# Seven half chunks of weights at another distance from the streamed tiles, and new paddings, in a two-block float32 network

## The chip, the cores and the metric

The kernel runs on one core of a Trainium2 chip. What counts is the device time of one execution in microseconds, the median of several runs. All times below are of that kind, or come from one profiled execution, in which they are counted from the start of its span.

## What is computed

Everything is float32, for one sequence of 256 tokens of width 1024. A first block (gated delta net, then a mixture of 16 experts) hands its normed result to a second block, which is the part that the change touches:

```python
def second_block(x, ...):
    for l in range(2):
        x = x + 0.5 * swiglu_ffn(rms_norm(x, g_ffn1[l]), w_up1[l], w_down1[l])
        h = rms_norm(x, g_mix[l])
        z = h @ w_in[l]          # z_lx, z_lg, q, k, v, f_logit, gates
        xr = causal_depthwise_conv(z_lx, conv_w[l], conv_b[l])
        hr = rg_lru(xr, w_a[l], b_a[l], w_x[l], b_x[l], lam[l])
        y_lru = (gelu(z_lg) * hr) @ w_lru_out[l]
        o = forgetting_attention(q, k, v, f_logit, g_q[l], g_k[l])
        y_attn = o @ w_attn_out[l]
        x = x + (gate_lru * y_lru + gate_attn * y_attn) @ w_o[l]
        x = x + 0.5 * swiglu_ffn(rms_norm(x, g_ffn2[l]), w_up2[l], w_down2[l])
    return x

def swiglu_ffn(h, w_up, w_down):       # w_up: 1024 x 5632, w_down: 2816 x 1024
    gate, up = split(h @ w_up, 2)
    return (silu(gate) * up) @ w_down
```

## The kernel before

**Three matmuls for one.** Each float32 operand is split into two fp32r parts, hi and lo, whose sum is the value. `mm3` (lines 238 to 243) issues three matmuls for every product of a 128x128 block of weights with 256 columns of activations: hi by hi (L241), lo weights by hi (L243 in the page, `mm<-xh,wlo`) and hi weights by lo (L242, `mm<-xl,whi`). The activations are the streamed (moving) operand, the weights are loaded. The scheduler issues the three in turn, so on TensorE nothing but such matmuls follow each other for long stretches.

**Weights.** They come in chunks of 128x2048 floats, 1 MB each, in the order that `order` gives: for each layer ffn1 (22 chunks `up1`, 11 of `down1`), the mix (`w_q`, `w_k`, `w_v`, `w_lx` for four groups, then `w_lg`, `w_g`, `w_la`, `w_o`), and ffn2 as ffn1. A chunk is loaded by one DMA on SyncE's queue into a `ring` of three, and `split` (L218) cuts it into two halves: for each, ScalarE writes `whi` (L228) and VectorE `wlo` (L229), from four places each. A half chunk feeds 24 matmuls. `weights` keeps two chunks ahead of their use. One ffn is 22 x 48 + 11 x 48 = 1584 matmuls.

**Streamed tiles.** `norm` writes `xh` (ScalarE, L254) and `xl` (VectorE, L255) per block of 128 channels, right after the residual add that makes this block (in w_o that is L726, `x<-mm,x`), and sums the squares on GpSimd (L259); a matmul with ones (L264, `ss<-sums,pack_base`) then gives the norm, behind the first chunk of the next stage. In ffn, `hh` and `hl` are the streamed tiles of `down`. In the mix, `w_lg` runs while the softmax of the last attention group is still worked on; its products go to one of three PSUM banks and L675 takes each out (`b<-mm,rstd`), which frees the bank for a later product.

**Other matmuls in fp32r.** `vproj` (L745 to L747) has the roles swapped: `xh` or `xl` is loaded and the weights are streamed. In `attention`, 8 matmuls for each of four groups (L566) spread the norms by `selt`, a matrix of zeros and ones that is the loaded operand. Some small products are in fp32: the scores (L579, L581: `qz`, `kz`) and `wax` (L646).

**Places.** The program fixes the address of every tile. `homed` pads the streamed tiles with 256 floats and lets them start 192 bytes into the padding; a padding `even` ahead of the pools sets the rest. Taken modulo 512, `xh`, `xl`, `hh`, `hl` and the streamed tiles of the mix all start at 352 and all `whi` and `wlo` at 160: weights 192 bytes below. For `vproj` it is the same pair the other way round. `selt` and `rn` lie at a distance of 128, `kz` and `qz`, `wax` and `xr` at 0.

**Order.** A scheduler lays out each engine's instructions from the dependencies and from when places come free. A new `whi` can be written when the last matmul that reads its place (four half chunks ago) is done.

Of the kernel before, what the change touches and what calls it, by code (L numbers as in the profile page):

```python
# [10 lines left out]
F32 = mybir.dt.float32  # L11
# [4 lines left out]
P = 128  # L16
T = 256
# [146 lines left out]

HOME, WEIGHTS = 192, 160


def homed(pool, n, dt, **kw):  # L170

    t = pool.tile([P, n * T + 256], dt, **kw)
    return t[:, HOME // 4:HOME // 4 + n * T].rearrange("p (k n) -> p k n", k=n)


class Kernel:
# [43 lines left out]
    def split(self, pool, raw, bufs=4, places=None):  # L220

        nc = self.nc
        parts = []
        for i in range(2):
            hi, lo = places[i]() if places else (pool.tile([P, 1024], F32R, tag=t, bufs=bufs, name=self.uid(t))
                                                 for t in ("whi", "wlo"))
            r = raw[:, 1024 * i:1024 * (i + 1)]
            nc.scalar.activation(hi, r, AF.Copy)  # L228
            nc.vector.tensor_sub(lo, r, hi.bitcast(F32))  # L229
            parts.append((hi, lo))  # L230

        def cols(n, size=P):
            i, o = divmod(n, 1024)
            return parts[i][0][:, o:o + size], parts[i][1][:, o:o + size]

        return cols
# [8 lines left out]
    def norm(self, x, g):  # L245

        nc, wp = self.nc, self.wp
        xh = homed(wp, KD, F32R, tag="xh", bufs=1, name=self.uid("xh"))
        xl = homed(wp, KD, F32R, tag="xl", bufs=1, name=self.uid("xl"))
        sums = wp.tile([P, T], F32, tag="sums", bufs=1, name=self.uid("sums"))  # L250

        def step(k):
            sq = wp.tile([P, T], F32, tag="t1", bufs=6, name=self.uid("sq")) if k else sums
            nc.scalar.activation(xh[:, k], x[:, k], AF.Copy, scale=self.c(g, k))  # L254
            nc.vector.scalar_tensor_tensor(xl[:, k], x[:, k], self.c(g, k), xh[:, k].bitcast(F32),  # L255
                                           op0=ALU.mult, op1=ALU.subtract)
            nc.scalar.activation(sq, x[:, k], AF.Square)
            if k:
                nc.gpsimd.tensor_add(sums, sums, sq)  # L259

        def finish():

            ss = self.ps.tile([P, 512], F32, tag="sm", bufs=2, name=self.uid("ss"))
            nc.tensor.matmul(ss[:, :T], self.cc["ones"], sums, start=True, stop=True)  # L264
            rms = wp.tile([P, T], F32, tag="t1", bufs=6, name=self.uid("rms"))
            nc.scalar.activation(rms, ss[:, :T], AF.Sqrt, bias=self.eps, scale=1.0 / D)
            rstd = wp.tile([P, T], F32, tag="rstd", bufs=2, name=self.uid("rstd"))
            nc.vector.reciprocal(rstd, rms)
            return rstd

        return ks(xh), ks(xl), step, finish

    def opening(self, x, f, g):

        nc, wp = self.nc, self.wp
        fg = self.wp1.tile([P, KD], F32, name="fg")
        nc.vector.tensor_mul(fg, self.cs(f), self.cs(g))

        by = self.wp1.tile([P, KD, 2], F32, name="by")
        nc.vector.memset(by[:, :, 0], 1.0)  # L280
        nc.vector.tensor_mul(by[:, :, 1], self.cs(f), self.cs(f))
        xh = homed(wp, KD, F32R, tag="xh", bufs=1, name=self.uid("xh"))
        xl = homed(wp, KD, F32R, tag="xl", bufs=1, name=self.uid("xl"))
        ss = self.ps.tile([P, 512], F32, tag="sm", bufs=2, name=self.uid("ss"))
        for k in range(KD):
            nc.scalar.activation(xh[:, k], x[:, k], AF.Copy, scale=fg[:, k:k + 1])
            nc.vector.scalar_tensor_tensor(xl[:, k], x[:, k], fg[:, k:k + 1], xh[:, k].bitcast(F32),
                                           op0=ALU.mult, op1=ALU.subtract)
            sq = wp.tile([P, T], F32, tag="t1", bufs=6, name=self.uid("sq"))
            nc.scalar.activation(sq, x[:, k], AF.Square)  # L290
            for t in range(2):
                nc.tensor.matmul(ss[:, 2 * t:2 * t + 2], sq[:, t * P:(t + 1) * P], by[:, k],
                                 start=(k == 0 and t == 0), stop=(k == KD - 1), skip_group_check=True)

        def spread(r):

            t = wp.tile([P, T], F32, tag="t1", bufs=6, name=self.uid("t"))
            tv = t.rearrange("p (t n) -> p t n", t=2)
            nc.vector.tensor_copy(tv, r[:, :, None].to_broadcast([P, 2, P]))
            b = self.ps.tile([P, 512], F32, tag="sm", bufs=2, name=self.uid("b"))  # L300
            for t in range(2):
                nc.tensor.matmul(b[:, t * P:(t + 1) * P], tv[:, t], self.cc["ident"], start=True, stop=True)
            return b[:, :T]

        def finish():
            sv = ss[:, :4].rearrange("p (t i) -> p i t", t=2)
            r = self.wp1.tile([P, 2, 2], F32, name="r")
            nc.scalar.activation(r[:, 0], sv[:, 0], AF.Sqrt, bias=self.eps, scale=1.0 / D)
            nc.vector.reciprocal(r[:, 0], r[:, 0])
            nc.vector.tensor_mul(r[:, 1], sv[:, 1], r[:, 0])  # L310
            nc.vector.tensor_mul(r[:, 1], r[:, 1], r[:, 0])
            nc.scalar.activation(r[:, 1], r[:, 1], AF.Sqrt, bias=self.eps, scale=1.0 / D)
            nc.vector.reciprocal(r[:, 1], r[:, 1])
            nc.vector.tensor_mul(r[:, 1], r[:, 1], r[:, 0])
            rstd = wp.tile([P, T], F32, tag="rstd", bufs=2, name=self.uid("rstd"))
            nc.scalar.activation(rstd, spread(r[:, 1]), AF.Copy)
            self.pending = residual(r[:, 0])
            return rstd

        def residual(r):  # L320
            rms = wp.tile([P, T], F32, tag="sums", bufs=1, name=self.uid("rms"))
            nc.scalar.activation(rms, spread(r), AF.Copy)
            for k in range(KD):
                yield
                nc.vector.scalar_tensor_tensor(x[:, k], x[:, k], self.c(f, k), rms, op0=ALU.mult, op1=ALU.mult)

        return ks(xh), ks(xl), None, finish

    def ffn(self, l, j, x, norm, g, out=None):

        nc, d = self.nc, self.d
        with ExitStack() as es:
            hp = self.pool("ffn", 1, ctx=es)
            xh, xl, _, finish = norm
            hh = homed(hp, FFT, F32R, name="hh")
            hl = homed(hp, FFT, F32R, name="hl")
            for m in range(FFT):
                w = self.weights(f"up{j}", l * FFT + m)
                pg = self.bank()
# [46 lines left out]
    def weights(self, name, i):  # L386

        while len(self.ahead) < 2:
            n = next(self.chunks, None)
            if n is None:  # L390
                break
            self.ahead.append((n, self.split(self.wp, self.load(self.d[n[0]][n[1]]))))
        n, w = self.ahead.pop(0)
        assert n == (name, i)
        return w
# [4 lines left out]
    def block2(self, x, out):  # L400
        nc = self.nc
        with ExitStack() as es:
            self.wp = self.pool("wp", 2, ctx=es)
            self.wp.tile([P, WEIGHTS // 4], F32, tag="even", bufs=1, name="even")
            self.ps = self.pool("ps", 1, True, ctx=es)
            self.wp1 = self.pool("wp1", 1, ctx=es)
            self.unpack("block2", self.wp1)
            self.selt = self.wp1.tile([P, 512], F32R, name="selt")

            self.wp1.tile([P, 64], F32, name="even")  # L410
            rows = self.cc["ident"].rearrange("p (n s) -> p n s", n=4)[:, :, :2]
            for n in range(4):
                nc.scalar.activation(self.selt[:, n * P:(n + 1) * P].rearrange("p (s c) -> p s c", c=64),
                                     rows[:, n, :, None].to_broadcast([P, 2, 64]), AF.Copy)
            self.chunks, self.ahead, self.pending = self.order(), [], iter(())
            norm = self.opening(x, "final_g", "g_ffn10")
            for l in range(LAYERS):
                norm = self.ffn(l, 1, x, norm, f"g_mix{l}")
                norm = self.mix(l, x, norm)
                norm = self.ffn(l, 2, x, norm, f"g_ffn1{l + 1}" if l + 1 < LAYERS else None, out)  # L420

    def mix(self, l, x, norm):
        nc, d, wp, ps = self.nc, self.d, self.wp, self.ps
        with ExitStack() as es:
            mp = self.pool("mix", 1, ctx=es)

            def big(i, dt=F32):
                return homed(mp, KD, dt, tag=f"b{i}", bufs=1, name=self.uid(f"b{i}"))

            def t1():  # L430
                return wp.tile([P, T], F32, tag="t1", bufs=6, name=self.uid("t"))
# [70 lines left out]
                tick()  # L502

            live.append(tokens())

            tmp("even", (P, 48))
            hr, lg = big(0), big(1)
            gh, gl, oh, ol = (big(i, F32R) for i in (2, 3, 4, 5))
            cv = [t.rearrange("(t two) n -> t two n", two=2) for t in (cum, ncum)]
# [1070 lines left out]
```

## Time and profile before

| what | us |
|---|---|
| median of three runs | 2606.05 |
| the three runs | 2598.6, 2606.05, 2613.8 |
| the profiled execution | 2613.88 |
| its span | 2612.2 |
| TensorE busy | 2255.4 (86%) |
| VectorE busy | 1203.8 (46%) |
| ScalarE busy | 982.7 (38%) |
| GpSimd busy | 278.9 (11%) |
| all `wlo` splits (460, VectorE) | 584.3 |
| all `whi` splits (460, ScalarE) | 484.6 |

The first block takes the first 1312 us or so; its second half is bound by the DMA of the experts' weights. Behind it, the second block runs at about half the DMA share. In the rows below a line reads: start in us, length in us, engine, line, operation, output<-inputs, and in brackets the idle time ahead of it with what ended it. Lengths of matmuls overlap, since TensorE is pipelined: the distance from start to start is what a matmul costs, and it is read from rows some places apart.

### The profile page before, as it was taken

To read this page: it belongs to the slowest core of one execution; us is meant where nothing else is said; L and a number is where in the kernel's file an instruction comes from. 1 tells how busy PE (TensorE), PEld (TensorE's weight loads), DVE (VectorE), ACT (ScalarE), POOL (GpSimd) and SP (SyncE) were. 2 spreads that over 40 slices of the span, in tenths; PEclk is the share of its full clock that TensorE was granted. 3 is DMA by queue.
4 is the path that set the end of the run, shared out by engine and by line. 5 is a ranking of instruction groups with operands and counts; after the bars stand their busy time and mean duration, and the time that the engine had idled before them with its cause. 6 is when DMAs were issued, how large, how long until landed. Compare 5 with 4: busy or idle time off the path is not lost.

```text
span 2612.2 us, 40963 instructions
## 1 busy us (share of the span) xinstructions
PE 2255.4 (86%) x17204; PEld 1701.6 (65%) x17204; DVE 1203.8 (46%) x1924; ACT 982.7 (38%) x1595; POOL 278.9 (11%) x349
## 2 busy tenths in 40 slices
PE   7999997666676666666699999999999999999999
PEld 3666883111122111111199988999999998899999
DVE  4797751000000000000065689866566568976654
ACT  4674651000000000000055567645445556665543
POOL 2442010000000000000011111101111121011110
PEclk9999998878788877888799999999999999999999
DMA  6246269999999999999945543455555553345553
GB/s 254 68 176 213 81 241 384 430 430 431 430 429 432 430 430 431 430 429 432 416 166 194 202 150 119 162 181 191 182 190 192 194 190 133 134 164 192 178 193 130
DMA packets 75160, 681.24 MB, mean 261 GB/s; under 512 B 10080, under 2 KB 13792, under 8 KB 15072
## 3 DMA queue, kind: packets, MB, share of 16 engines
q1 hardware_dynamic: 71920, 677.48, 65.8%
q8 instruction: 135, 2.21, 0.3%
q10 hardware_dynamic: 3056, 1.15, 0.2%
q14 instruction: 49, 0.40, 0.0%
HBM read 677.47 MB, written 1.05 MB: 260 GB/s over the span
## 4 chain that ended last, share of the span: by engine, by line
PE 48%; DMA 35%; DVE 11%; ACT 3%; issue 2%; POOL 1%; ACTq 0%; SPq 0%; DVEq 0%; POOLq 0%; another core or an unknown queue 0%
PE mm L241 14%; PE mm L242 14%; PE mm L243 13%; DMA arena<-e_down 10%; DMA arena<-e_gate 6%; DMA arena<-e_up 4%; DMA expert_ring<-e_gate 4%; DVE wlo L229 3%; DMA ring<-e_up 3%; DMA expert_ring<-e_down 3%; DMA ring<-e_down 1%; DMA expert_ring<-e_up 1%; DMA ring<-e_gate 1%; DVE xr L636 1%; DMA early_zs<-w_mod 1%
## 5 line engine op out<-in xcount | busy, mean ns | idle before, releaser
L229 DVE TENSOR_TENSOR wlo<-ring,whi 128x1024 fp32r<-128x1024 f32 x460 | 584.3, 1273 | 307.8 <-ACT whi L228 307.5
L228 ACT ACTIVATE whi<-ring 128x1024 fp32r<-128x1024 f32 x460 | 484.6, 1056 | 399.2 <-PE mm L242 342.8
L241 PE MATMUL mm<-xh,whi 128*128 128x256 f32 x2176 | 613.4, 282 | 10.7 <-DVE kk L522 7.4
L243 PE MATMUL mm<-xh,wlo 128*128 128x256 f32 x2176 | 610.9, 281 | 0.0
L242 PE MATMUL mm<-xl,whi 128*128 128x256 f32 x2176 | 609.7, 280 | 0.2
L241 PEld LDWEIGHTS mm<-xh,whi 128*128 128x128 f32 x2176 | 412.5, 190 | 16.0 <-issue 6.8
L243 PEld LDWEIGHTS mm<-xh,wlo 128*128 128x128 f32 x2176 | 414.2, 190 | 0.3
L242 PEld LDWEIGHTS mm<-xl,whi 128*128 128x128 f32 x2176 | 411.2, 189 | 1.0 <-DVE xl L255 0.6
L930 DVE TENSOR_TENSOR hid<-hid,u 128x512 f32<-128x512 f32 x16 | 11.0, 688 | 505.7 <-PE u L926 505.7
L241 PE MATMUL mm<-hh,whi 128*128 128x256 f32 x704 | 196.1, 278 | 0.0
L242 PE MATMUL mm<-hl,whi 128*128 128x256 f32 x704 | 196.1, 278 | 0.0
L243 PE MATMUL mm<-hh,wlo 128*128 128x256 f32 x704 | 196.1, 278 | 0.0
L926 PE MATMUL u<-arena,xs 128*32 128x512 f32 x608 | 105.4, 823 | 73.3 <-DMA arena<-e_up 73.3
L952 DVE COPY y<-x 128x512 f32<-128x512 f32 x16 | 11.1, 692 | 309.2 <-PE x L947 309.2
L243 PEld LDWEIGHTS mm<-hh,wlo 128*128 128x128 f32 x704 | 133.7, 190 | 0.0
L242 PEld LDWEIGHTS mm<-hl,whi 128*128 128x128 f32 x704 | 132.1, 188 | 0.0
L241 PEld LDWEIGHTS mm<-hh,whi 128*128 128x128 f32 x704 | 132.1, 188 | 0.0
L352 POOL TENSOR_TENSOR hl<-hid,hh 128x256 fp32r<-128x256 f32 x88 | 68.5, 778 | 555.5 <-ACT hh L351 555.5
L938 ACT ACTIVATE ht<-x 128x512 f32<-128x512 f32 x16 | 9.6, 597 | 310.0 <-PE x L936 310.0
L926 PEld LDWEIGHTS u<-arena,xs 128*32 128x32 f32 x608 | 19.5, 130 | 160.0 <-DMA arena<-e_up 124.5
L926 PE MATMUL g<-arena,xs 128*32 128x512 f32 x640 | 83.4, 647 | 41.5 <-DMA arena<-e_gate 41.5
L947 PE MATMUL d<-arena,ht 128*32 128x512 f32 x304 | 75.5, 777 | 47.2 <-DMA arena<-e_down 42.2
(513 smaller groups left out, 3796.1 us busy)
## 6 DMA issues: line engine op xcount, KB each, us to landing
ring<-up SPq DMA_DIRECT2D x88, 1024.0 KB, 4.8
arena<-e_gate SPq DMA_DIRECT2D x40, 2048.0 KB, 34.2
arena<-e_up SPq DMA_DIRECT2D x38, 2048.0 KB, 35.1
arena<-e_down SPq DMA_DIRECT2D x38, 2048.0 KB, 34.3
ring<-down SPq DMA_DIRECT2D x44, 1024.0 KB, 4.8
expert_ring<-e_down SPq DMA_DIRECT2D x20, 2048.0 KB, 34.0
expert_ring<-e_up SPq DMA_DIRECT2D x19, 2048.0 KB, 34.1
expert_ring<-e_gate SPq DMA_DIRECT2D x18, 2048.0 KB, 34.0
```

The source lines that it names most:

```text
L228: nc.scalar.activation(hi, r, AF.Copy)
L229: nc.vector.tensor_sub(lo, r, hi.bitcast(F32))
L241: mm(out, ah, bh, start=start, stop=False)
L242: mm(out, ah, bl, start=False, stop=False)
L243: mm(out, al, bh, start=False, stop=stop)
L352: nc.gpsimd.tensor_sub(hl[:, m], hid, hh[:, m].bitcast(F32))
L636: nc.vector.scalar_tensor_tensor(xr, lx[:, j:j + T], cw(j), xr, op0=ALU.mult, op1=ALU.add)
L926: nc.tensor.matmul(gu[s][32 * q:32 * q + 32], xs[:, k, ec], w[:, 512 * q:512 * q + 512], start=(k == 0), stop=(k == KD - 1))
L930: nc.vector.tensor_mul(hid, hid, gu[1])
L938: nc.scalar.activation(ht, xb, AF.Copy)
L947: nc.tensor.matmul(dn[n][32 * q:32 * q + 32], ht[:, i * P + 32 * q:i * P + 32 * q + 32], ws[q][:, o:o + 512], start=(i == 0), stop=(i == 3))
L952: nc.vector.tensor_copy(y[1], dn[1])
```

## The change

Three things change, all of them in where tiles lie.

1. `homed` goes. The streamed tiles are plain tiles and paddings of 88, 80, 64 and two times 48 floats (`gap0`, `gap1`, `GAP1`, `gap2`, `GAP2`) set the places. As before, all weights from the four shared places lie 192 bytes below the streamed tiles modulo 512.
2. Two new places, `ahi` and `alo` (4 KB a partition each), at distance 0 modulo 512 from the streamed tiles.
3. Seven half chunks are split into these places instead of the shared ones: the first halves of `up1` 2 and 6, `up2` 2 and `w_g` 0 in layer 0, and of `up1` 24, `w_g` 8 and `up2` 24 in layer 1. That is 7 x 24 = 168 matmuls. The second halves stay in the shared places.

```diff
-HOME, WEIGHTS = 192, 160
-
-
-def homed(pool, n, dt, **kw):
-
-    t = pool.tile([P, n * T + 256], dt, **kw)
-    return t[:, HOME // 4:HOME // 4 + n * T].rearrange("p (k n) -> p k n", k=n)
+ASIDE = [("up1", 2), ("up1", 6)] + [("up2", 2)] + [("up1", FFT + 2), ("up2", FFT + 2)] + [("w_g", KD * l) for l in range(LAYERS)]
+
+GAP1, GAP2 = 64, 48
...
-            hi, lo = places[i]() if places else (pool.tile([P, 1024], F32R, tag=t, bufs=bufs, name=self.uid(t))
-                                                 for t in ("whi", "wlo"))
+            hi, lo = places[i]() if places and places[i] else (
+                pool.tile([P, 1024], F32R, tag=t, bufs=bufs, name=self.uid(t)) for t in ("whi", "wlo"))
...
-        xh = homed(wp, KD, F32R, tag="xh", bufs=1, name=self.uid("xh"))
-        xl = homed(wp, KD, F32R, tag="xl", bufs=1, name=self.uid("xl"))
+        xh = wp.tile([P, KD, T], F32R, tag="xh", bufs=1, name=self.uid("xh"))
+        xl = wp.tile([P, KD, T], F32R, tag="xl", bufs=1, name=self.uid("xl"))
...
-            self.ahead.append((n, self.split(self.wp, self.load(self.d[n[0]][n[1]]))))
+            places = None
+            if n in ASIDE:
+                if n == ASIDE[0]:
+                    self.wp.tile([P, 48], F32, tag="gap2", bufs=1, name="gap2")
+                ahi, alo = (self.wp.tile([P, 1024], F32R, tag=t, bufs=1, name=self.uid(t)) for t in ("ahi", "alo"))
+                places = [lambda: (ahi, alo), None]
+            self.ahead.append((n, self.split(self.wp, self.load(self.d[n[0]][n[1]]), places=places)))
...
-            self.wp.tile([P, WEIGHTS // 4], F32, tag="even", bufs=1, name="even")
+
+            self.wp.tile([P, 88], F32, tag="gap0", bufs=1, name="gap0")
...
-            self.wp1.tile([P, 64], F32, name="even")
+            self.wp1.tile([P, GAP1], F32, name="gap")
...
+            self.wp.tile([P, 80], F32, tag="gap1", bufs=1, name="gap1")
...
-            tmp("even", (P, 48))
+            tmp("gap", (P, GAP2))
```

On TensorE the order stays, but the weights of these half chunks have another name. Here is the end of the second chunk and the start of the third of ffn2 in layer 0, before (the number behind a name is the tile's):

```order
L241 MATMUL mm_12037<-xh_11660,whi_11961 128x256
L242 MATMUL mm_12037<-xl_11661,whi_11961 128x256
L243 MATMUL mm_12037<-xh_11660,wlo_11962 128x256
L241 MATMUL mm_12103<-xh_11660,whi_12029 128x256
L242 MATMUL mm_12103<-xl_11661,whi_12029 128x256
L243 MATMUL mm_12103<-xh_11660,wlo_12030 128x256
```

And the same place after:

```order
L237 MATMUL mm_12039<-xh_11662,whi_11963 128x256
L238 MATMUL mm_12039<-xl_11663,whi_11963 128x256
L239 MATMUL mm_12039<-xh_11662,wlo_11964 128x256
L237 MATMUL mm_12105<-xh_11662,ahi_12029 128x256
L238 MATMUL mm_12105<-xl_11663,ahi_12029 128x256
L239 MATMUL mm_12105<-xh_11662,alo_12030 128x256
```

The 24 matmuls of this half chunk now read `ahi` and `alo`; nothing is moved.

The new places are free when the shared ones are not, so the split of such a half chunk can come earlier. VectorE at the end of w_o in layer 0, before (`x` is the residual add, `xl` the streamed lo part):

```order
L726 TENSOR_TENSOR x<-mm_11846,x 128x256
L229 TENSOR_TENSOR wlo_11884<-ring_11877,whi_11883 128x1024
L255 SCALAR_TENSOR_TENSOR xl_11661<-x,pack_base,xh_11660 128x256
L726 TENSOR_TENSOR x<-mm_11887,x 128x256
L229 TENSOR_TENSOR wlo_11958<-ring_11955,whi_11957 128x1024
L255 SCALAR_TENSOR_TENSOR xl_11661<-x,pack_base,xh_11660 128x256
L726 TENSOR_TENSOR x<-mm_11918,x 128x256
```

The same place after:

```order
L728 TENSOR_TENSOR x<-mm_11848,x 128x256
L225 TENSOR_TENSOR wlo_11886<-ring_11879,whi_11885 128x1024
L251 SCALAR_TENSOR_TENSOR xl_11663<-x,pack_base,xh_11662 128x256
L225 TENSOR_TENSOR alo_12030<-ring_12031,ahi_12029 128x1024
L728 TENSOR_TENSOR x<-mm_11889,x 128x256
L225 TENSOR_TENSOR wlo_11960<-ring_11957,whi_11959 128x1024
L251 SCALAR_TENSOR_TENSOR xl_11663<-x,pack_base,xh_11662 128x256
L728 TENSOR_TENSOR x<-mm_11920,x 128x256
```

The `alo` of ffn2's third chunk has come ahead of the last two residual adds; before, the `wlo` of that half chunk stood behind the reciprocal of the norm. ScalarE's `ahi` comes ahead likewise. Layer 1 has the same.

VectorE in `w_lg` of layer 0, before (`b` takes a product out of its PSUM bank, `nm` and `smx` belong to the softmax of the last attention group):

```order
L675 TENSOR_TENSOR b_1169_8630<-mm_10311,rstd_8676 128x256
L589 TENSOR_REDUCE nm_10266<-s_10338 128x2
L229 TENSOR_TENSOR wlo_10382<-ring_10375,whi_10381 128x1024
L675 TENSOR_TENSOR b_1169_8630<-mm_10385,rstd_8676 128x256
L595 RECIPROCAL smx_10267<-smx_10267 128x8
```

The same place after:

```order
L677 TENSOR_TENSOR b_1169_8632<-mm_10313,rstd_8678 128x256
L591 TENSOR_REDUCE nm_10268<-s_10340 128x2
L225 TENSOR_TENSOR wlo_10384<-ring_10377,whi_10383 128x1024
L225 TENSOR_TENSOR alo_10540<-ring_10541,ahi_10539 128x1024
L677 TENSOR_TENSOR b_1169_8632<-mm_10387,rstd_8678 128x256
L597 RECIPROCAL smx_10269<-smx_10269 128x8
```

The `alo` of `w_g` 0 now stands ahead of the second `b`. Layer 1 has the same with `w_g` 8. SyncE's DMAs and GpSimd keep their order; on TensorE one `wax` matmul of each layer comes nine places earlier.

## Rows read from the trace of the kernel before

**Rows 1.** The page: span, and busy time by engine.

```profile
span 2612.2 us, 40963 instructions
PE 2255.4 (86%) x17204; PEld 1701.6 (65%) x17204; DVE 1203.8 (46%) x1924; ACT 982.7 (38%) x1595; POOL 278.9 (11%) x349
```

**Rows 2.** Windows: stretch, its us, TensorE busy (matmuls), granted clock, DMA share, GB/s.

```profile
1360.00:1500.00 140.00, 140.00 (x1237) 1.00 0.55 194
1664.50:1754.70 90.20, 90.20 (x768) 1.00 0.53 187
1790.00:1965.00 175.00, 175.00 (x1488) 1.00 0.53 187
1970.00:2140.00 170.00, 170.00 (x1503) 1.00 0.55 193
2310.10:2400.30 90.20, 90.20 (x768) 1.00 0.53 187
2435.60:2608.00 172.40, 172.40 (x1466) 1.00 0.49 171
```

**Rows 3.** Groups by line: L242 in 1360 to 1500, then 1790 to 1930; busy, mean.

```profile
L242 PE MATMUL mm<-xl,whi 128*128 128x256 f32 x236 | 65.1, 276 | 0.0
...
L242 PE MATMUL mm<-xl,whi 128*128 128x256 f32 x313 | 88.0, 281 | 0.0
```

**Rows 4.** Timeline of TensorE at the start of ffn2 in layer 0.

```profile
1776.65 0.28 PE L241 MATMUL mm<-xh,whi 128*128 128x256 f32 x1
...
1777.33 0.28 PE L241 MATMUL mm<-xh,whi 128*128 128x256 f32 x1
1778.05 0.70 PE L264 MATMUL ss<-sums,pack_base 128*128 128x256 f32 x2 [0.45 <-POOL sums L259]
...
1778.70 0.28 PE L243 MATMUL mm<-xh,wlo 128*128 128x256 f32 x1
...
1779.41 0.28 PE L243 MATMUL mm<-xh,wlo 128*128 128x256 f32 x1
```

**Rows 5.** Timeline of TensorE around the first group of `selt` matmuls.

```profile
1527.35 1.11 PE L566 MATMUL s<-rn,selt 128*128 128x256 f32 x8
1528.29 0.28 PE L241 MATMUL mm<-xh,whi 128*128 128x256 f32 x1
...
1528.65 0.28 PE L241 MATMUL mm<-xh,whi 128*128 128x256 f32 x1
...
1530.13 0.28 PE L242 MATMUL mm<-xl,whi 128*128 128x256 f32 x1
```

**Rows 6.** Timeline of TensorE where the v projection (L745 to L747) ends.

```profile
1553.14 0.28 PE L747 MATMUL mm<-whi,xl 128*128 128x256 f32 x1
...
1553.93 0.28 PE L241 MATMUL mm<-xh,whi 128*128 128x256 f32 x1
...
1554.64 0.28 PE L241 MATMUL mm<-xh,whi 128*128 128x256 f32 x1
```

**Rows 7.** Timeline of TensorE: fp32 scores, and what follows them.

```profile
1568.46 1.89 PE L581 MATMUL s<-kz,qz 128*128 128x256 f32 x8
1570.19 0.59 PE L646 MATMUL mm<-xr,wax 128*128 128x256 f32 x2
```

**Rows 8.** Timelines of VectorE and of ScalarE (last row) at the end of w_o.

```profile
1771.89 0.96 DVE L255 SCALAR_TENSOR_TENSOR xl<-x,pack_base,xh 128x256 fp32r<-128x256 f32 x1
...
1773.46 1.23 DVE L229 TENSOR_TENSOR wlo<-ring,whi 128x1024 fp32r<-128x1024 f32 x1 [0.28 <-ACT whi L228]
...
1777.33 0.95 DVE L255 SCALAR_TENSOR_TENSOR xl<-x,pack_base,xh 128x256 fp32r<-128x256 f32 x1
...
1772.36 1.07 ACT L228 ACTIVATE whi<-ring 128x1024 fp32r<-128x1024 f32 x1 [0.94 <-ACT sq L257]
```

**Rows 9.** Timelines of VectorE and of TensorE (last row) in w_lg.

```profile
1643.56 0.42 DVE L675 TENSOR_TENSOR b<-mm,rstd 128x256 f32<-128x256 f32 x1
...
1644.03 0.39 PE L241 MATMUL mm<-xh,whi 128*128 128x256 f32 x1 [0.73 <-DVE b L675]
```

More of the change, by code (lines that the diff above doesn't have):

```diff
@@ L281, in opening @@
         nc.vector.tensor_mul(by[:, :, 1], self.cs(f), self.cs(f))
-        xh = homed(wp, KD, F32R, tag="xh", bufs=1, name=self.uid("xh"))
-        xl = homed(wp, KD, F32R, tag="xl", bufs=1, name=self.uid("xl"))
+        xh = wp.tile([P, KD, T], F32R, tag="xh", bufs=1, name=self.uid("xh"))
+        xl = wp.tile([P, KD, T], F32R, tag="xl", bufs=1, name=self.uid("xl"))
         ss = self.ps.tile([P, 512], F32, tag="sm", bufs=2, name=self.uid("ss"))
@@ L334, in ffn @@
             xh, xl, _, finish = norm
-            hh = homed(hp, FFT, F32R, name="hh")
-            hl = homed(hp, FFT, F32R, name="hl")
+            hh = hp.tile([P, FFT, T], F32R, name="hh")
+            hl = hp.tile([P, FFT, T], F32R, name="hl")
             for m in range(FFT):
@@ L427, in big @@
             def big(i, dt=F32):
-                return homed(mp, KD, dt, tag=f"b{i}", bufs=1, name=self.uid(f"b{i}"))
+                return mp.tile([P, KD, T], dt, tag=f"b{i}", bufs=1, name=self.uid(f"b{i}"))
             def t1():
```

## The prediction

> **What bounds the kernel now.** I read the page first, for the shares: of the span of 2612.2 us TensorE is busy 2255.4 us, 86% [rows 1]. The first half, to about 1312 us, is the same code before and after; the change lives in the second half. There I read the windows next, and the reader should look at three columns: PE busy equals the length of the window, the granted clock is 1.00 (the upper of the two levels, 2.4 GHz), and the DMA share is near a half [rows 2]. So in these stretches nothing is waited for: TensorE's own pace sets the time, and the only thing that could shorten them is the distance in time from one matmul to the next.
>
> The fourth column, the count, shows that this pace has two values. All of these matmuls have one shape (128x128 weights, 256 columns, fp32r). In 1360 to 1500 and 1970 to 2140 they come at (140.00 + 170.00) / (1237 + 1503) = 113.1 ns; in the other four windows at (90.20 + 175.00 + 90.20 + 172.40) / (768 + 1488 + 768 + 1466) = 527.8 / 4490 = 117.55 ns. The groups by line say the same in another number: one matmul lasts 276 ns in the first kind of stretch and 281 in the second [rows 3]; they overlap, and all three lines (hi by hi, hi by lo, lo by hi) change together. I call the paces short and long. They differ by 4.4 ns, 4%.
>
> What makes a stretch long? Not the place of the tiles: ffn1 and ffn2 take the same places of weights, 192 bytes below the same streamed tiles modulo 512, and in both layers ffn1 is short and ffn2 long. Not the clock, which is 1.00 in all. The timeline shows when the pace changes: at a disturbance. At the start of ffn2 in layer 0, six matmuls take 0.68 us up to 1777.33, then the ones matmul waits 0.45 us for GpSimd, and from 1778.70 on six take 0.71 us [rows 4], and so on to the end of the pass, 187 us later. Between disturbances I found no change of pace within a run of one distance. So each pass draws its pace at its last disturbance and keeps it: this is a state, and the question is what sets it.
>
> **What the seven half chunks meet.** Each is the first half chunk of weights after the last disturbance ahead of a long quiet run: 24 matmuls whose weights lie at distance 0. In the trace of before they would stand at 1329.5, 1351.8 (ffn1, layer 0), 1661.7 (w_g), 1787.3 (ffn2), and in layer 1 at 1974.6, 2307.3 and 2432.9 us. The four long windows of [rows 2] begin where such a half chunk ends. No fp32r matmul of before stands at distance 0, so what it does must be judged from rows at other distances.
>
> The nearest that there is to a kick in the trace: eight matmuls with `selt` as weights, which lie at distance 128, between matmuls at the usual distance. They take 0.94 us; the three that follow come 120 ns apart (1528.29 to 1528.65), and the thirteen after those 113.8 ns [rows 5], short. All 8 groups of that line end so, whichever pace stood before them. The other kind: the v projection swaps the roles (the streamed tile becomes the weights), which makes the distance 192 the other way round; where it hands over without a gap, at 1553.93, the pace goes from 0.79 us for seven (113 ns) to 0.71 us for six (118 ns) [rows 6]; of eight such changes six end long and two short. So a change of distance does reset the state, and which way depends on the distance that is left.
>
> **Part 1, the pace after a half chunk at distance 0.** I take it that it works like `selt`: the run that follows is short. Then the 4490 matmuls of the four long windows go from 117.55 to 113.1 ns: 4490 x 4.4 = 19.8 us saved (3.4 + 6.6 + 3.4 + 6.5 by window). The first two and the fifth half chunk stand in passes that are short already: nothing to gain there in this execution, though in others they may be long.
>
> **Part 2, the 168 matmuls at distance 0 themselves.** Lower end: eight fp32 matmuls whose two tiles are at distance 0 take 1.73 us from 1568.46 to 1570.19 [rows 7], 216 ns each, and fp32 passes the data twice, so 108 ns a pass. Of the 168, 72 (three half chunks in ffn1) come at 113.1 ns now and 96 at 117.55: 72 x -5.1 + 96 x -9.5 = -1.3 us. Upper end: the 120 ns behind `selt` [rows 5], 72 x 6.9 + 96 x 2.5 = +0.7 us. I take the 117.5 of the eight `selt` matmuls (0.94 / 8), the nearest in type: 72 x 4.4 = +0.3 us.
>
> **Part 3, the split that moves.** The new places are free early, so the scheduler puts the split of the aside half earlier on VectorE and ScalarE (the order of before and after shows it). At the end of w_o, `alo` now stands between the `xl` of 1771.89 and the `x` behind it. One step lasts 2.72 us there (half of 1771.89 to 1777.33, the last `xl`) and VectorE idles only 0.28 us in it [rows 8]. A `wlo` takes 1.23. Two idles of 0.28 swallow 0.56, so the last `xl` and the sums come 0.7 us later (0 if the gaps elsewhere give, 1.2 if none does), and TensorE, which waits there for 0.45 us already [rows 4], waits that much more; queued behind it on VectorE are the last two residual adds, on ScalarE their `xh`. Two layers: +1.4 us. The matching `ahi` on ScalarE fits the 0.94 us idle [rows 8]: free; if its DMA were late, the `whi` behind it would be. In w_lg, `alo` of w_g now stands ahead of the `b` of line 675, whose PSUM bank TensorE waits 0.73 us for [rows 9] with nothing else ready; the softmax's last steps are queued behind it. The whole 1.2 us comes on top, twice: +2.4 us. In ffn1, three banks lie between the split and its use and VectorE has slack: nothing; without that cover 1.2 us each. Sum +3.8 (0 to 4.9). The other tiles move by some bytes with the one distance kept; the unused paddings cost no instruction: nothing.
>
> **The sum.** The profiled execution took 2613.88 us, the highest of the three; the median is 2606.05. 2613.9 - 19.8 + 0.3 + 3.8 = **2598.2 us**. A run with one long ffn pass more or less differs by 1584 x 4.4 = 7 us, which is the distance between the three times: I take the median to be a draw with one more pass short. So the sum is made from the profiled time, where I know which stretches are long, and not from the median; with all long runs short the draw is gone.
>
> **The rivals.** *A, forecast:* 2598 us, 2593 (waits 0, lower end of part 2: 2592.8) to 2600 (all upper ends: 2599.7). Some 1050 long matmuls in q, k, v and lx stand outside my windows; if those turn short too it is up to 4.6 us less, and if stretches of the mix that are short now turn long, some us more: 2592 to 2602. *B, distance 0 sets nothing*, the pace is drawn anew by stalls as before. For it: after 64 disturbances in the trace 35 runs are short and 29 long, nearly a coin. Against it: the 8 of 8 behind `selt` [rows 5]. Time: the median with parts 2 and 3, 2606 + 4 = 2610 us, 2602 to 2618 by a pass more or less. *C, distance 0 hands over long*, as the v projection does in six of eight [rows 6]. Then the passes that are short now turn long: from the second half chunk of ffn1 in layer 0, 1295 x 4.4 = 5.7, and in layer 1 1487 x 4.4 = 6.6 us: 2613.9 + 12.3 + 4.1 = 2630.3 us, slower. It decides from the one point of which pace follows the 24 matmuls. Against it: distance 0 in fp32 shows no conflict [rows 7], and a pace that leaves the run at 108 to 118 ns comes from the short side.
>
> The rows show that spacing depends on the distance (113 or 118 at the usual one, 117.5 and 120 around `selt`). The Trainium skill ("SBUF — State Buffer", section "Who interferes with whom") says that only the port pair shared by VectorE and GpSimd causes contention, and that TensorE reads weights and streamed tile by two independent ports: by that rule distances could change nothing, and the change would be parts 2 at zero and 3 alone, 2610 us, which is B's time. The trace agrees with it only so far as one distance carries both paces.
>
> **How the numbers follow.** A 0.62, B 0.23, C 0.15. About 0.5% is what a measurement of this kernel can tell from no change: 2593.0 and 2619.1 us. Below 2593.0 lies a sixth of A (q, k, v short too, or no wait from part 3): faster 0.10. C and the top of B are slower: 0.16. The rest, 0.74, is the same. Range: A whole and most of B, 2592 to 2616; A's own is 2592 to 2602.
>
> **What would show it.** Right: in ffn2 and w_g windows of after 276 ns a matmul and some 1546 matmuls where 1488 fit into 175 us; in both ffn1 still 276; at the 168 matmuls with `ahi` and `alo` a spacing between 108 and 120; TensorE's wait at the ffn2 start up from 0.45 to about 1.1, and at `b` from 0.73 to about 1.8. Part 1 is wrong by B if any long run after a half chunk at distance 0 stays at 281 while another is at 276, by C if all are at 281. Part 3 is wrong if these waits are unchanged.

## The result: slower by 0.6%, because the half chunks make the pace long

| | before | after |
|---|---|---|
| median us (12 runs each) | 2611.32 | 2626.14 |
| lowest to highest | 2598.6 to 2619.73 | 2623.35 to 2628.57 |
| profiled execution, us | 2613.88 | 2628.08 |
| ratio of the times | | 1.0058, 95% interval 1.0044 to 1.0072 |

The forecast was 2598 us; rival C, at 2630 us against the profiled 2613.88, is what happened. The runs also lie closer together: 5 us from end to end, where those of before take 21.

The page of after gives little: TensorE is busy 9 us longer in a span that is 14 us longer, with the same number of matmuls [rows 1].

```profile
span 2626.3 us, 40958 instructions
PE 2264.1 (86%) x17204; PEld 1715.2 (65%) x17204; DVE 1203.6 (46%) x1926; ACT 982.7 (37%) x1593; POOL 277.7 (11%) x349
```

The windows of after show it. The columns are the stretch, its us, TensorE busy (matmuls), the granted clock, the DMA share and GB/s. The stretches answer to those of [rows 2] in their order: ffn1 and w_g and ffn2 of layer 0, then of layer 1.

```profile
1360.00:1500.00 140.00, 140.00 (x1191) 1.00 0.53 187
1671.00:1760.00 89.00, 89.00 (x758) 1.00 0.52 188
1797.00:1970.00 173.00, 173.00 (x1471) 1.00 0.52 183
1985.00:2155.00 170.00, 170.00 (x1445) 1.00 0.52 181
2324.00:2410.00 86.00, 86.00 (x733) 1.00 0.52 183
2450.00:2620.00 170.00, 170.00 (x1446) 1.00 0.48 169
```

Divide time by count: 117.5, 117.4, 117.6, 117.6, 117.3, 117.6 ns. All six are long. Both ffn1, which were short at 113.1 [rows 2], are long now: that of layer 0 holds 1191 matmuls in 140 us where 1237 fitted. The granted clock is 1.00 throughout, as before, so the clock is not it. The groups of 1360 to 1500 in after say the same by the length of a matmul, 281 ns where [rows 3] has 276:

```profile
L238 PE MATMUL mm<-xl,whi 128*128 128x256 f32 x236 | 66.3, 281 | 0.0
```

The timeline of TensorE in after, around the half chunk of ffn2 in layer 0 (start in us, length, engine, line, operation), shows the moment. The names with `a` are the 24 matmuls at distance 0.

```profile
1793.09 0.28 PE L237 MATMUL mm<-xh,whi 128*128 128x256 f32 x1
...
1793.77 0.28 PE L237 MATMUL mm<-xh,ahi 128*128 128x256 f32 x1
...
1796.53 0.28 PE L239 MATMUL mm<-xh,alo 128*128 128x256 f32 x1
1796.65 0.28 PE L237 MATMUL mm<-xh,whi 128*128 128x256 f32 x1
...
1797.35 0.28 PE L237 MATMUL mm<-xh,whi 128*128 128x256 f32 x1
```

Six matmuls ahead of it take 0.68 us, 113 ns each: this stretch was short. Inside, 23 steps take 2.76 us, 120.0 ns each. Behind it, six take 0.70 us, about 117, and the 1485 that follow without a disturbance are 117.8 ns apart on average. So here the half chunk turned a short run into a long one. The run behind is long at all seven: four of them met a short run, one a long run, and the two of w_g stand directly behind other matmuls.

By stage, from the first matmul of one to the first of the next in the two profiled executions: ffn1 186.6 to 194.1 us in layer 0 and 180.7 to 187.4 in layer 1, together +14.2; w_lg 30.7 to 32.1 and 32.2, +2.9; q, k, v and lx 132.3 and 133.3 to 130.6 and 131.8, -3.2; w_g, w_o and ffn2 together +1.2; the start of ffn1 0.9 us earlier. The sum is +14.2, as the two executions differ. The q, k, v stage gives no gain that belongs to the change: in the ten other profiles below, the same code took from 130.5 to 133.7 us there, and before and after lie inside that. The 0.8 us by which w_g and w_o of layer 1 grew do not belong to it either: w_o ran at the long pace there (191 long matmuls, 24 in layer 0), and in the second execution of the changed kernel below it did not.

### The profile page after: what moved, and what is told of

It reads as the page before. It is cut to its first block, busy times and chain, and to the rows that moved or that the text cites. A ratio compares the mean times of both kernels' runs of the same rounds, so it can differ in the third digit from the quotient of the medians.

```text
span 2626.3 us, 40958 instructions
## 1 busy us (share of the span) xinstructions
PE 2264.1 (86%) x17204; PEld 1715.2 (65%) x17204; DVE 1203.6 (46%) x1926; ACT 982.7 (37%) x1593; POOL 277.7 (11%) x349
## 4 chain that ended last, share of the span: by engine, by line
PE 49%; DMA 34%; DVE 10%; ACT 3%; issue 2%; POOL 1%; ACTq 0%; SPq 0%; DVEq 0%; POOLq 0%
PE mm L237 14%; PE mm L238 14%; PE mm L239 14%; DMA arena<-e_down 10%; DMA arena<-e_gate 6%; DMA arena<-e_up 4%; DMA expert_ring<-e_gate 4%; DMA ring<-e_up 3%; DVE wlo L225 3%; DMA expert_ring<-e_down 3%; DMA ring<-e_gate 1%; DMA ring<-e_down 1%; DMA expert_ring<-e_up 1%; DMA early_zs<-w_mod 1%; DVE xr L638 1%
## 5 line engine op out<-in xcount | busy, mean ns | idle before, releaser
L225 DVE TENSOR_TENSOR wlo<-ring,whi 128x1024 fp32r<-128x1024 f32 x453 | 574.6, 1271 | 300.1 <-ACT whi L224 299.2
L224 ACT ACTIVATE whi<-ring 128x1024 fp32r<-128x1024 f32 x453 | 476.6, 1055 | 404.1 <-PE mm L238 346.2
L237 PE MATMUL mm<-xh,whi 128*128 128x256 f32 x2120 | 599.1, 283 | 13.7 <-DVE kk L524 7.5
L239 PE MATMUL mm<-xh,wlo 128*128 128x256 f32 x2120 | 597.0, 282 | 0.0
L238 PE MATMUL mm<-xl,whi 128*128 128x256 f32 x2120 | 595.9, 281 | 0.0
L237 PEld LDWEIGHTS mm<-xh,whi 128*128 128x128 f32 x2120 | 406.0, 192 | 18.6 <-issue 6.5
L238 PEld LDWEIGHTS mm<-xl,whi 128*128 128x128 f32 x2120 | 399.6, 188 | 0.7 <-DVE xl L251 0.4
L239 PEld LDWEIGHTS mm<-xh,wlo 128*128 128x128 f32 x2120 | 399.4, 188 | 0.3
```

The lines of the kernel that those rows point to most:

```text
L237: mm(out, ah, bh, start=start, stop=False)
L238: mm(out, ah, bl, start=False, stop=False)
L239: mm(out, al, bh, start=False, stop=stop)
```

## Experiments

**Does the distance decide, and which way?** Four variants of the changed kernel keep its early splits, and in their traces VectorE, ScalarE and GpSimd do the same instructions in the same order as in the changed kernel. Only the padding ahead of `ahi` changes, with the rest of 512 bytes behind `alo`, so that nothing else moves. Two come here and two further down. Each ratio below is against executions of before taken together with that variant, whose medians lay between 2606.0 and 2609.3 us. The edit:

```diff
-self.wp.tile([P, 48], F32, tag="gap2", bufs=1, name="gap2")
+self.wp.tile([P, 48 + DIST // 4], F32, tag="gap2", bufs=1, name="gap2")
 ahi, alo = (self.wp.tile([P, 1024], F32R, tag=t, bufs=1, ...) for t in ("ahi", "alo"))
+if n == ASIDE[0]:
+    self.wp.tile([P, 128 - DIST // 4], F32, tag="gap3", bufs=1, name="gap3")
```

With DIST = 320, the distance that all other weights have:

> The changed kernel with the seven half chunks in their own places, but at distance 320, as all other weights: what is left of the change is the earlier splits and the moved paddings. Theory: without a change of distance the half chunks set nothing, the pace is drawn by the stalls ahead as in the kernel before, and the waits (+1.4 us in w_lg per layer) and the q, k, v stage (-1.6 us per layer) cancel: 2600 to 2620 us, with differences of about 7 us between runs. Rival (the earlier splits or the paddings make the time): 2626 us, as the changed kernel.

Measured: 2606.14 us, 2598.13 to 2626.72; 0.9995 of before (0.9972 to 1.0017). The loss is gone and the wide spread is back. So neither the earlier splits nor the paddings make the 15 us.

With DIST = 128, where `selt` lies:

> The changed kernel with the seven half chunks at distance 128 modulo 512 instead of 0; order and splits as in the changed kernel. Theory (the distance that is left sets the pace of the run behind it, and 128 hands over short, as behind selt in the kernel before): all seven long runs go short, so that of the 8550 long matmuls of the changed kernel some 7400 come at 113.3 instead of 117.8 ns: 2626.1 - 7400 x 4.45 ns = 2593 us. Rival 1 (every change of distance hands over long, as it did 7 of 7 times after 0): 2626 us. Rival 2 (selt hands over short for another reason than its distance): the pace behind is drawn, 2605 to 2622 us.

Measured: 2600.82 us, 2596.49 to 2605.66; 0.9961 of before (0.9948 to 0.9975). Rival 1 is out. The theory holds behind five half chunks of the seven and fails in w_g. The windows of this kernel for w_g, ffn2 and ffn1 of layer 1:

```profile
1666.00:1752.00 86.00, 86.00 (x733) 1.00 0.52 183
1793.00:1955.00 162.00, 162.00 (x1432) 1.00 0.54 189
1975.00:2130.00 155.00, 155.00 (x1370) 1.00 0.54 191
```

113.1 ns in ffn2 and ffn1, 117.3 in w_g of layer 0 (and of layer 1). Two w_g stretches of 765 matmuls at 4.4 ns are 6.8 us, most of the 8 us by which the time missed the 2593 that was expected. So 128 does not hand over short from every pace, and the eight `selt` groups of [rows 5] were a narrower witness than I took them for: in the trace of before two of them follow a short run, six follow other matmuls of the attention, and none meets a long run. The time of rival 2 was not met either, but its condition is not out: `selt` may hand over short for another reason than its distance.

**A map of distances.** One profiled execution of a kernel in which 60 half chunks, 15 per ffn, lie aside in one tile, each at its own offset:

```diff
+ASIDE = dict(zip(SITES, DIST))     # the first halves of every second chunk; 0, 128, 0, 64, 0, 192, ...
...
+o = ASIDE[n] // 4
+both = self.wp.tile([P, 2048 + 128], F32R, tag="aside", bufs=1, ...)
+ahi, alo = both[:, o:o + 1024], both[:, o + 1024:o + 2048]
```

> The changed kernel with 60 half chunks aside, 15 in each ffn pass (first halves of every second chunk), each at its own distance: multiples of 32 between 0 and 480 modulo 512, most of them twice, once behind a half chunk at 0 and once behind one at 128. Theory: the pace behind a half chunk depends on its distance alone: long after 0, short after 128, and each other distance gives one of the two, whichever pace came before. Rival (a toss at each change): at one distance both paces follow. The time itself says nothing: 2590 to 2630 us.

The windows of this kernel below are 8 us long, each behind a half chunk. Since a matmul that is still running is counted at both ends, 70 or 71 in a window means long and 73 short. In order: behind 0 (short before it), 64 (long before), 192 (long), 256 (long), 448 (long), 64 (short), 256 (short), 32 (long), 32 (short).

```profile
1332.60:1340.60 8.00, 8.00 (x70) 1.00 0.47 182
1366.80:1374.80 8.00, 8.00 (x71) 1.00 0.49 180
1389.50:1397.50 8.00, 8.00 (x73) 1.00 0.50 184
1411.90:1419.90 8.00, 8.00 (x70) 1.00 0.48 173
1462.90:1470.90 8.00, 8.00 (x73) 1.00 0.46 172
1809.00:1817.00 8.00, 8.00 (x73) 1.00 0.56 197
...
1852.80:1860.80 8.00, 8.00 (x71) 1.00 0.50 190
1993.00:2001.00 8.00, 8.00 (x70) 1.00 0.48 169
2455.60:2463.60 8.00, 8.00 (x73) 1.00 0.52 192
```

All sites read in the same way, with the spacing of the 24 matmuls themselves (the mean of the 23 steps between them):

| distance (modulo 512) | ns a matmul inside | pace behind it, back at 320 |
|---|---|---|
| 0, 256 | 120.0 | long, from either pace |
| 32, 288 | 118.3 to 118.4 | as before |
| 64, 320 | 113.3 or 117.8, as before | as before |
| 96, 352 | 120.1 from short, 117.4 from long | short |
| 128, 384 | 118.3 to 118.7, uneven | short from short; from long, either |
| 160, 416 | 119.9, uneven | short |
| 192, 448 | 113.3 or 117.8, as before | short |
| 224, 480 | 116.7 to 116.8, uneven | short (480 met a short run only) |

The table repeats after 256 in each row. So the rival (a toss) falls for all distances but 128 and 384, and my theory was too narrow: some distances set the pace and some keep it. Most pairs of distance and pace stand on one half chunk each in this one execution; 0 stands on 17. The next runs test two rows of the table on whole kernels.

It is the distance between the two operands that counts, and not the place of the weights alone. The v projection of the changed kernel loads `xl` and `xh`, which lie at the same place modulo 512 as `ahi` and `alo`, but streams weights 192 bytes from them. Its matmuls come at both paces and not at 120.0; here six take 0.68 us, 113 ns each:

```profile
1559.61 0.28 PE L749 MATMUL mm<-whi,xl 128*128 128x256 f32 x1
...
1560.29 0.28 PE L749 MATMUL mm<-whi,xl 128*128 128x256 f32 x1
```

**256 as a second 0.** The same edit with DIST = 256:

> The changed kernel with the seven half chunks at distance 256 modulo 512 instead of 0. The map repeats after 256 (two half chunks at 256 were 120 ns apart a matmul inside and left a long pace, like those at 0). Theory: so 256 is as 0: 120 ns inside, long behind all seven, 2626 us within 3. Rival (only 0, the very same place modulo 512, sets long; the two half chunks of the map were chance): drawn, 2600 to 2620 us.

Measured: 2627.38 us, 2624.82 to 2629.8; 1.0076 of before (1.0048 to 1.0103). The half chunks are as far as can be from the streamed tile's own place modulo 512, and the result is that of distance 0, with 120.0 ns inside and a long run behind all seven. Its window of ffn2 in layer 0 (117.6 ns):

```profile
1797.00:1960.00 163.00, 163.00 (x1386) 1.00 0.54 187
```

**192, which should cure.** DIST = 192:

> The changed kernel with the seven half chunks at distance 192 modulo 512 instead of 0. In the map, the run behind 192 (and 448) was short from either pace, and the 24 matmuls themselves kept the pace they met. Theory (the distance left sets the pace, 192 always short): short in all seven runs, w_g too, which stayed long at 128: 2600.8 - 2 x 765 x 4.45 ns = 2594 us, range of the runs no wider than 10 us. Rival (at 192 the pace is drawn and the map showed two lucky pairs): some stretch behind a half chunk stays long, 2600 us or more.

Measured: 2594.68 us, 2591.66 to 2600.41; 0.9954 of before (0.9937 to 0.9970). The timeline of TensorE in this kernel at the end of the half chunk in ffn2 of layer 0, where a long run met it:

```profile
1790.64 0.28 PE L240 MATMUL mm<-xh,alo 128*128 128x256 f32 x1
...
1791.11 0.28 PE L238 MATMUL mm<-xh,whi 128*128 128x256 f32 x1
...
1791.79 0.28 PE L238 MATMUL mm<-xh,whi 128*128 128x256 f32 x1
```

Four matmuls take 0.47 us (117.5 ns) up to the change and six take 0.68 (113) after it. The windows of w_g of both layers, which 128 had left long, are short here: 82 us for 726 matmuls, 113 ns.

```profile
1669.00:1751.00 82.00, 82.00 (x726) 1.00 0.53 190
...
2307.00:2389.00 82.00, 82.00 (x726) 1.00 0.53 189
```

**The same cure without places of its own.** The kernel before, with all second halves 128 bytes higher, so that every chunk goes from 320 to 448 and the next one back:

```diff
+if two and i and not self.padded:
+    pool.tile([P, 32], F32, tag="pad1", bufs=1, name="pad1")
 hi, lo = places[i]() if places else (
-    pool.tile([P, 1024], F32R, tag=t, bufs=bufs, ...) for t in ("whi", "wlo"))
+    pool.tile([P, 1024], F32R, tag=t + "b" * (two and i), bufs=bufs // (1 + two), ...) for t in ("whi", "wlo"))
+if two and i and not self.padded:
+    self.padded = pool.tile([P, 96], F32, tag="pad2", bufs=1, name="pad2") is not None
```

> The kernel before with no half chunk aside: the first half of every chunk stays at distance 320, the second half of every chunk goes 128 bytes higher, to 448 (two places each instead of four shared; the order on all engines stays). Theory: the pace turns short at each change from 448 to 320 and is kept at each change back, so that a long pace lives for at most a chunk and nearly all of the 5543 long matmuls of the kernel before turn short: its profiled 2613.9 - 5300 x 4.45 ns = 2590 us, with runs within 6 us of each other. Rival (a change can set long as well): 2600 to 2620 us.

Measured: 2593.91 us, 2587.15 to 2596.71; 0.9947 of before (0.9926 to 0.9968). The long stretches are short, as this window of its w_g shows (81 us for 717, 113 ns). The median misses the expected 2590 us by 4, and the spread is 9.6 us where 6 was expected. About 1150 long matmuls are left in its profile, two thirds of them in the q, k, v stages around the v projection, where the expectation had 240. They are worth 4 us, but they do not account for the miss: the execution in which they were counted took 2590.42 us. What made it 4 us shorter elsewhere, and the median longer, is open.

```profile
1663.00:1744.00 81.00, 81.00 (x717) 1.00 0.56 195
```

**Is the pace a draw, then?** The kernel before and the changed one each once more.

> The kernel before once more, for a second profile. Theory (each stretch draws its pace at its last stall): the stretches that are long differ from those of the first profile, and the time follows their count at 4.45 ns a matmul. Rival (the pace belongs to the stage): ffn1 short, ffn2 and w_g long again, and the time differs for another reason.

> The changed kernel once more, for a second profile. Theory: every run behind a half chunk at distance 0 is long again, 7 of 7, and the time is within 3 us of 2626.

Before once more took 2604.17 us. Its windows of w_g, ffn2 and ffn1 in layers 0, 0 and 1:

```profile
1663.00:1749.00 86.00, 86.00 (x733) 1.00 0.53 185
1790.00:1950.00 160.00, 160.00 (x1414) 1.00 0.55 197
1965.00:2130.00 165.00, 165.00 (x1404) 1.00 0.53 187
```

ffn2 is short here (113.2 ns) and ffn1 of layer 1 long (117.5), the reverse of [rows 2]; w_g is long as it was. So the pace of an ffn pass is not a property of its stage: the two executions of one kernel differ in three of its four ffn passes. It has 4101 long matmuls where the first profile has 5543: 1442 x 4.4 = 6.4 us of the 9.7 between the two. The changed kernel once more took 2627.64 us, with the same six long windows (1191, 758, 1471, 1446, 733 and 1446 matmuls). So where nothing at another distance stands, the pace of an ffn pass is drawn, and behind a half chunk at 0 it is not.

**One part alone.** Only w_g and ffn2 keep their half chunks at 0; ffn1 uses the shared places.

```diff
+FEW = [n for n in ASIDE if n[0] != "up1"]
-places = [lambda: (ahi, alo), None]
+places = [lambda: (ahi, alo), None] if n in FEW else None
```

> The changed kernel with only four of the seven half chunks at distance 0 (w_g and ffn2 of both layers); the three of ffn1 go to the shared places. Theory: the 14 us that the two ffn1 passes lost come back wherever their stalls draw short, and ffn2 and w_g stay long by force: 2608 to 2616 us. Rival (the cost lies in w_g, ffn2 or their waits): 2624 us or more.

Measured: 2622.84 us, 2613.72 to 2627.43; 1.0052 of before (1.0035 to 1.0069), a miss for the theory, and 1 us short of the rival. The profile says why it is no proof for either: ffn1 came back short in layer 0, but in layer 1 it drew long by itself (1404 matmuls in 165 us, 117.5 ns).

```profile
1360.00:1495.00 135.00, 135.00 (x1193) 1.00 0.55 195
...
1985.00:2150.00 165.00, 165.00 (x1404) 1.00 0.54 188
```

I had counted only against the first profile of before, in which w_g and ffn2 were long anyway; against executions that draw ffn2 short, forcing it long costs up to 14 us.

**What the moved splits cost, and the best kernel.** The kernel with distance 192, its half chunks in w_g and ffn2 one chunk later:

```diff
-ASIDE = [("up1", 2), ("up1", 6)] + [("up2", 2)] + [("up1", FFT + 2), ("up2", FFT + 2)] + [("w_g", KD * l) for l in range(LAYERS)]
+ASIDE = [("up1", 2), ("up1", 6)] + [("up2", 3)] + [("up1", FFT + 2), ("up2", FFT + 3)] + [("w_g", KD * l + 1) for l in range(LAYERS)]
```

> The kernel with the seven half chunks at distance 192, but in w_g and ffn2 one chunk later (w_g 1 and 9, up2 3 and 25), so that their split no longer stands ahead of the last products of w_lg and of the residual adds of w_o. Theory: w_lg goes back from 32.1 to 30.7 us in each layer and the ffn2 start by 0.4 us; one more chunk of w_g and ffn2 (48 matmuls) may stay long, up to 4 x 0.2 us: 2594.7 - 3.6 + 0.8 = 2592 us, and the traces show w_lg at 30.7. Rival (the wait in w_lg has another cause than the moved split): w_lg stays at 32.1 and the time at 2594.7.

Measured: 2590.62 us, 2588.14 to 2594.0; 0.9931 of before (0.9904 to 0.9957), the lowest median of all; its interval overlaps those of the kernel with 192 and of the one with two distances. In w_lg, TensorE waits as in [rows 9] again, and the stage takes 30.8 us; the start of ffn2 in layer 0 waits 0.45 us, as in [rows 4]. So the rival (another cause than the moved split) is out. First the timeline of the changed kernel (distance 0) there, of VectorE:

```profile
1648.73 1.23 DVE L225 TENSOR_TENSOR alo<-ring,ahi 128x1024 fp32r<-128x1024 f32 x1
1649.86 0.43 DVE L677 TENSOR_TENSOR b<-mm,rstd 128x256 f32<-128x256 f32 x1
```

Of TensorE there (in brackets the idle time and what ended it):

```profile
1650.34 0.38 PE L237 MATMUL mm<-xh,whi 128*128 128x256 f32 x1 [2.10 <-DVE b L677]
```

And TensorE at the same place in this kernel, whose `alo` comes later:

```profile
1642.52 0.39 PE L238 MATMUL mm<-xh,whi 128*128 128x256 f32 x1 [0.71 <-DVE b L680]
```

The wait is 2.10 us with `alo` ahead of `b`, and 0.71 without; before it was 0.73.

## Why the prediction was wrong

**What bounds the kernel** was right: two paces at one clock, kept from one disturbance to the next, 4.4 ns apart. After's six windows carry the long one of the same two numbers. A line through the profiled time and the count of long matmuls of the twelve profiles has a slope of 4.5 ns a matmul; the times span 38 us, and single profiles lie up to 6 us off the line. So the count is the main term, and not the only one.

**The step that failed is part 1**, where I took distance 0 to work like `selt`, which lies at 128. It has another effect: long, from either pace. I had said that which way a reset goes depends on the distance that is left, and then borrowed the way from another distance because that row was of the same kind of matmul. Nothing in the trace of before showed an fp32r run at 0, so the honest weight was near even between A and C, and not 0.62 to 0.15. The reading of [rows 5] was wrong too: that all eight groups ended short "whichever pace stood before them" is not in the trace, where two met a short run and none a long one. The traces above do have two groups that met a long run, in the kernel with two distances, and they ended short as well; a half chunk at 128 does that only sometimes, so `selt` does not stand for 128 either.

**The witness for C was underrated too, and partly misread.** The v projection [rows 6] hands over at 192 in name, and 192 hands over short in the kernel with the half chunks there. But the v projection swaps the roles: its last matmul streams a `whi` while the next one's weights, another `whi`, are loaded, and those two lie at distance 0 modulo 512. That reading, by which the load and the stream that run at the same time count, fits its long hand-overs. In the eleven profiles in which all shared weights lie at one distance, there are 88 such hand-overs: all 44 that met a short pace left a long one, and of those that met a long one 22 left it long and 22 short. These last 22 are no toss: they are the first v projection of each layer, in all eleven profiles. The reading does not explain them. Nor does it explain the kernel with two distances, where the two tiles at the hand-over lie 128 apart and not 0: all eight hand-overs left a long pace there too, one of them from a short one, which neither 64 (their distance in name) nor 128 did in the map. So why the v projection hands over long is open.

**The sum of C**, by its terms: ffn1 +5.7 and +6.6 were +7.5 and +6.7 from start to start of the stages. In layer 0 the first half chunk already turned 120 matmuls, which I had left out, and the second half chunk's own matmuls add some; the rest of that stage's difference is not taken apart, and the two executions of the changed kernel themselves differ there by 1.6 us (194.1 and 192.5). **Part 2** was +0.3 with 117.5 ns inside; the matmuls at 0 come at 119.9 to 120.0, so 72 x 6.8 + 96 x 2.4 = +0.7 us, the upper end. The fp32 row [rows 7] was no guide, and I misread it: line 581 issues four matmuls a group and the row has x8, so one fp32 matmul is two records of 216 ns, and that such a record is two passes of 108 ns is not in the trace. Nothing in it speaks of an fp32r matmul at the same distance. **Part 3** was right in kind and nearly in size. In w_lg I had +1.2 us a layer and the wait grew from 0.73 to 2.10 in layer 0 and to 2.19 in layer 1, +1.4 and +1.5. At the start of ffn2 I had +0.7 and it was +0.34 in layer 0, as TensorE's row there shows against [rows 4] (0.45); in layer 1, behind a w_o at the long pace, it was +0.07.

```profile
1784.83 0.70 PE L260 MATMUL ss<-sums,pack_base 128*128 128x256 f32 x2 [0.79 <-POOL sums L255]
```

Together 3.2 us of the 3.8 predicted, but not the reason for the result.

**The rule that I cited as a rival** (the Trainium skill, "SBUF — State Buffer", section "Who interferes with whom") does not hold for these matmuls. With the weights of 24 matmuls moved by some bytes, at equal order and clock, the pace of the run behind them changes by 4%. What in the chip makes the distance count, no run here shows. The page "TensorE: Matmul & The Clock Gate" of the Trainium skill, section "Step-by-step: what each phase is for", says likewise that loading the next weights does not take read bandwidth from the running matmul; a spacing of 120.0 ns at distance 0, where 320 allows 113.3, speaks against that as well.

**The spread.** I took the profile's 7.8 us above the median for one long pass more. That fits: a second profile of before, 9.7 us shorter, had one long pass fewer, and the count of long matmuls gives 6.4 us of it. What stays open is what decides the draw at a stall, and why w_g came out long in both layers of all four profiles in which no half chunk stood in it or none at another distance (two of before, the one at 320 and the map).

## What to carry to other kernels

When the same matmuls at full clock come at two spacings, first look for what the operands' addresses have to do with it: put a few dozen of them at each distance in one kernel and read spacing inside and behind. A row at one address distance is no evidence for another one; if the trace does not hold the case, weigh both signs alike. Once the table is known, the cure can be cheap: two places for the weights at distances that reset to the short pace (320 and 448 here) cost no instruction and no place in the order.

## What the runs showed of the hardware

- fp32r matmuls of 128x128 weights and 256 columns run back to back at the granted clock 1.00 in 113.3, 117.8 or 120.0 ns, by the distance in bytes between loaded and streamed operand and by what came before. At 320 modulo 512 both 113.3 and 117.8 keep themselves up, for 1485 matmuls and more; at 64, 192 and 448 each was kept over the 24 matmuls that were tried; at 0 and 256 there is only 120.0.
- The dependence repeats after 256 bytes, not 512, in all eight rows of the map.
- A change back to 320 from 0 or 256 left 117.8 in all 44 cases; from 96, 160, 192, 224 and their like 256 bytes further it left 113.3 in all but one of some 200 cases without a disturbance near them (most of them in the kernel with two distances, where the pace was short already; the exception is there too, in w_o).
- The VectorE split that a free place let the scheduler move up cost 1.1 to 1.5 us of TensorE's time where a PSUM bank was waited for (waits of 1.86 to 2.19 us in the two executions of the changed kernel, against 0.73), and 0.34 us where 0.57 us of idle time stood in its queue.
